# Row-prefix sums of eight batches: one static part for all batches, a ring of three instead of four, shorter programs

## The chip, the cores and the metric

One core of a Trainium2 chip runs the kernel. Its time is the device time of one execution, in microseconds (us). Five runs of the kernel before were timed; one further execution was taken by the hardware profiler, and all views below are of that one.

## The reference

```python
B, S, D = 8, 8192, 512                     # x: float32 [B, S, D], w: float32 [D, D]
mask = (pos < lengths[:, None, None])
cs = np.cumsum(x * mask, axis=1)
midpoints = (lengths // 2).clip(0)
mid_features = cs[b_idx, midpoints, :]      # one row per batch
return np.matmul(mid_features[:, None, :], w).squeeze(1)
```

Only one row of the running sum is used per batch, so what has to be computed is the sum of the rows 0 to min(length // 2, length - 1) of each batch, and then a product of eight rows with w. The lengths are data: the kernel learns at run time how many rows each batch needs. In the draw that is timed they are 1138, 5379, 511, 4113, 1809, 7542, 7716 and 1140, so that half of each is 569, 2689, 255, 2056, 904, 3771, 3858 and 570.

## The kernel before

The sum over rows is a matrix product. A chunk is a tile of 128 partitions, each with U = 8 consecutive rows of some batch (a unit, 16 KB). For each of the 8 rows (a slab, u) TensorE multiplies the tile's 128 x 512 values with a 128 x 8 table of ones and zeros, which says to which batch the partition's row belongs and whether it counts. The products of all chunks are added up in one PSUM bank, `s_ps`, in four groups of columns (32 j), one for every fourth slab. They are folded together at the end.

Rows come in three ways. The *front* (L519) is static: rows 0 to 255 of all batches, two parts of four batches with 2 MB each, issued by SP before anything is known of the lengths, into slots 0 and 1 of the ring `xt`. The *gathers* are dynamic: POOL's `fetch` (L244) loads by a table of unit numbers, `idx`, one chunk of 128 units (2 MB) at a time. A unit number that is out of range moves no bytes. The *back* (L281, `xb`) is static again: rows 256 to 511 of batches 0 and 1, loaded at the end. So batches 0 and 1 begin their gathered rows at 512 and the other six at 256; the rows `least`, `extra`, `jump` and `shift` carry this difference through the arithmetic on DVE (L317 to L329). The last gather goes in two halves to a buffer of its own, `xl`.

The order at the start, on DVE (`vector`, L297): constants, then from the lengths a row of unit counts (`row`), which PE spreads over the partitions by a product with ones (L441, `bc_ps`); from that the table of unit numbers (`ge`, `z`, `idx`) for all C = 31 possible chunks; then a second row (`row2`) and its spread (`b2_ps`), the weights of the front, and the weights `wc` of all chunks (`early`, `wc`). PE (`tensor`, L427) first writes zeros into its PSUM banks by products with a row of zeros (L437).

The steady state is a ring of R = 4 slots. SP relays (`relay`): once a slot's weights (`s_wr`) and its gather (`s_full`) are there it raises `s_rdy`, on which PE waits. After a chunk's eight products PE raises `s_done`. On that, POOL (`gather`, L266) copies the next column of `idx` into `now` and issues the next gather into the freed slot, and ACT (`weigh`) copies the next chunk's weights into `wr`. Behind each chunk PE runs two idle products (L449), whose result nobody reads. The front parts stand in slots 0 and 1, the first two gathers go to slots 2 and 3 without waiting for any chunk.

At the end POOL issues the two halves of the last chunk, `xb` and `w` in this order (L279 to L288), on one queue. PE (`pe_end`, L472) adds the last chunk, then `xb` into `c_ps` (two batches, quarter by quarter of the columns), folds `s_sb` into `mf_ps` (L495, four products), adds `c_sb` by a product with `pick` (L498), and multiplies by w (`o_ps`). DVE and ACT copy the result out; SP and ACT store it. PE's program has `pe_end` first in memory, then 56 waits that are met at once (`pe_pad`), then its start.

Every DVE operation is recorded at L301, all of PE's slab products at L429; the tile names tell them apart.

Of the kernel before, what the change touches and what calls it, by code (L numbers as in the profile page):

```python
# [8 lines left out]
I32 = mybir.dt.int32  # L9
# [6 lines left out]
def kernel(  # L16
# [13 lines left out]

    nc = tc.nc
# [5 lines left out]
    R = 4  # L37
    UB = S // U
    HEAD = 256
    FRONT = 2  # L40
    FB = B // FRONT
    BB = 2
    BU = 2
    BACK = slice(HEAD, HEAD + P * BU)
    HU, BKU = HEAD // U, (BACK.stop - HEAD) // U
# [3 lines left out]
    PAD = 56  # L49
    HALF = 2  # L50
    UH = U // HALF
    xu = x.rearrange("b (q u) d -> (b q) (u d)", u=U)
    xh = x.rearrange("b (q u) d -> (b q) (u d)", u=UH)
# [10 lines left out]
    def sem(name):  # L64
# [3 lines left out]
    xl = sb("xl", [P, HALF, UH * D])  # L68
    xb = sb("xb", [P, BB, BU * D])
    wt = sb("wt", [P, KC, D])  # L70
    lens = sb("lens", [1, 2 * B], I32)
    l16 = sb("l16", [1, B], I32)
    l2 = sb("l2", [1, B], I32)
    least = sb("least", [1, B])
    extra = sb("extra", [1, B])
    jump = sb("jump", [1, B - 1])
    shift = sb("shift", [1, B])
    last = sb("last", [1, B])
# [5 lines left out]
    chunks = sb("chunks", [1, 1], I32)  # L84
    ones = sb("ones", [1, P])
    zero = sb("zero", [1, D])
    p_i = sb("p_i", [P, 1], I32)
    p4 = sb("p4", [P, 1], I32)
    base = sb("base", [P, 1], I32)
    rank = sb("rank", [P, 1])  # L90
    rank8 = sb("rank8", [P, 1])
    q_i = sb("q_i", [P, C], I32)
    v_i = sb("v_i", [P, C * U], I32)
    u_i = sb("u_i", [P, U], I32)
    h_i = sb("h_i", [P, FB], I32)
    h_f = sb("h_f", [P, FB], I32)
    off_f = sb("off_f", [P, FB])
    at_f = sb("at_f", [P, FB])
    v_f = sb("v_f", [P, U, FB])
    v_b = sb("v_b", [P, BU], I32)  # L100
    v8 = sb("v8", [P, C * U])
# [3 lines left out]
    idx_h = sb("idx_h", [P, HALF], I32)  # L105
    now = sb("now", [P, R], I32)
    early = sb("early", [P, C, U, B])
    wc = sb("wc", [P, C, U * B])
    wr = sb("wr", [P, R * U * B])
    wl = sb("wl", [P, U * B])  # L110
    wb = sb("wb", [P, BB, BU, BB])
    fold_i = sb("fold_i", [P, B], I32)
    fold_m = sb("fold_m", [P, B], I32)
    fold = sb("fold", [P, B])
    pick_i = sb("pick_i", [P, KC, BB], I32)
    pick = sb("pick", [P, KC, B])
    s_sb = sb("s_sb", [P, D])
    c_sb = sb("c_sb", [P, P])
# [4 lines left out]
    c_ps = ps("c_ps", [P, D])  # L123
    mf_ps = ps("mf_ps", [P, KC * B])
    o_ps = ps("o_ps", [P, D])
# [5 lines left out]
    s_front = [sem(f"front{k}") for k in range(FRONT)]  # L131
    s_last = [sem(f"last{k}") for k in range(HALF)]
    s_back = [sem(f"back{k}") for k in range(BB)]
    s_w = [sem(f"w{k}") for k in range(4)]
    s_len, s_out, s_pool, s_dve, s_pe, s_done, s_wr, s_rdy, s_zero, s_act, s_wl, s_now = (
        sem(n) for n in ("len", "out", "pool", "dve", "pe", "done", "wr", "rdy", "zero", "act", "wl", "now"))
# [3 lines left out]
    QUARTERS = [slice(0, D // 2, 2), slice(1, D // 2, 2), slice(2 * P, 3 * P), slice(3 * P, D)]  # L140
    W_AT = (0, 2)

    def weights_of(s):
        return wr[:, s * U * B:(s + 1) * U * B]
# [12 lines left out]
    def sync(sp):  # L157
# [5 lines left out]
        sp.wait_ge(s_dve, marks["chunks"])  # L163
        sp.load(left, chunks[:])
        sp.wait_ge(s_dve, marks["front"])
        for f in range(FRONT):
            sp.wait_ge(s_front[f], 16)
            sp.sem_inc(s_rdy, 1)
        sp.br(f"sy_0_{FRONT}")

        def relay(s):
            sp.wait_ge(s_wr, have)
            sp.wait_ge(s_full[s], full)
            sp.sem_inc(s_rdy, 1)
            sp.reg_add(have, have, 1)
            if s == FRONT - 1:
                sp.reg_add(full, full, 16)

        ring(sp, "sy", left, relay)
        with nc.body("sy_end", valid_engines=[sp.engine]):  # L180
            sp.wait_ge(s_dve, marks["out0"])
            sp.wait_ge(s_act, 1)
            store(sp, 0)
            sp.br(END)


    def scalar(act):
        act.memzero(xl[:]).then_inc(s_zero, 1)  # L188
        left = act.alloc_register("left_act")
        free = act.alloc_register("free_act")  # L190
        act.wait_ge(s_dve, marks["w"])
        act.load(left, count[:])
        act.reg_sub(left, left, 1)
        last = act.snap(left)
        act.copy(out=wl[:], in_=wc[:, bass.ds(last, 1)].rearrange("p c e -> p (c e)"),
                 ).then_inc(s_wl, 1)
        act.reg_add(left, left, FRONT)
        for s in range(FRONT, R):
            act.copy(out=weights_of(s), in_=wc[:, s - FRONT]).then_inc(s_wr, 1)
        act.reg_sub(left, left, R)  # L200
        act.reg_mov(free, 1)
        act.br("ac_0_0")

        def weigh(s):
            act.wait_ge(s_done, free)
            col = act.snap(free)
            act.copy(out=weights_of(s),  # L207
                     in_=wc[:, bass.ds(col + (R - FRONT - 1), 1)].rearrange("p c e -> p (c e)"),
                     ).then_inc(s_wr, 1)
            act.reg_add(free, free, 1)  # L210

        ring(act, "ac", left, weigh)
        with nc.body("ac_end", valid_engines=[act.engine]):
            for g in range(2):
                act.wait_ge(s_pe, 6 + g)
                act.copy(out=o_sb[64 * g:64 * g + B, P:], in_=o_ps[64 * g + 32:64 * g + 32 + B, :P],  # L216
                         ).then_inc(s_act, 1)
            act.wait_ge(s_act, 2)
# [8 lines left out]
    def gpsimd(pool):  # L227
        pool.iota(p_i[:], pattern=[[0, 1]], base=0, channel_multiplier=1).then_inc(s_pool, 1)
        pool.wait_ge(s_pool, 1)
        for k in range(4):  # L230
            pool.iota(base[32 * k:32 * k + 32], pattern=[[0, 1]],
# [3 lines left out]
        pool.iota(q_i[:], pattern=[[P, C]], base=0, channel_multiplier=0).then_inc(s_pool, 1)  # L235
        pool.iota(h_i[:], pattern=[[-1, FB]], base=4 * FB, channel_multiplier=1)
        pool.iota(u_i[:], pattern=[[1, U]], base=0, channel_multiplier=0)
        pool.iota(v_i[:], pattern=[[P * U, C], [1, U]], base=HEAD, channel_multiplier=0)
        pool.iota(v_b[:], pattern=[[1, BU]], base=BACK.start, channel_multiplier=BU)
        pool.iota(fold_i[:], pattern=[[-1, B]], base=128, channel_multiplier=1)  # L240
        pool.iota(pick_i[:], pattern=[[-32, KC], [-1, BB]], base=0, channel_multiplier=1,
# [8 lines left out]
        n = pool.alloc_register("n_pool")  # L250
        free = pool.alloc_register("free_pool")
        pool.wait_ge(s_dve, marks["idx"])
        pool.load(n, count[:])
        pool.reg_sub(n, n, 1)
        pool.reg_mov(free, 1)
        pool.br("gp_a_0")
        for c in range(R - FRONT):
            with nc.body(f"gp_a_{c}", valid_engines=[pool.engine]):
                pool.br_cmp(n, c, f"gp_b_{c}", "gp_end", "IS_GT")
            with nc.body(f"gp_b_{c}", valid_engines=[pool.engine]):  # L260
                fetch(xt[:, c + FRONT], xu, idx[:, c:c + 1], B * UB, s_full[c + FRONT])
                if c + 1 == R - FRONT:
                    pool.reg_sub(n, n, R - FRONT)
                pool.br(f"gp_a_{c + 1}" if c + 1 < R - FRONT else "gp_0_0")

        def gather(s):  # L266
            pool.wait_ge(s_done, free)
            col = pool.snap(free)
            pool.tensor_copy(out=now[:, s:s + 1], in_=idx[:, bass.ds(col + (R - FRONT - 1), 1)],  # L269
                             ).then_inc(s_now, 1)  # L270
            pool.sem_inc(s_now, -1)._wait_ge(s_now, 1)  # L271
            fetch(xt[:, s], xu, now[:, s:s + 1], B * UB, s_full[s])
            pool.reg_add(free, free, 1)  # L273

        ring(pool, "gp", n, gather)
        with nc.body("gp_end", valid_engines=[pool.engine]):
            pool.wait_ge(s_zero, 1)
            pool.wait_ge(s_dve, marks["idx_h"])
            for h in range(HALF):  # L279
                fetch(xl[:, h], xh, idx_h[:, h:h + 1], B * S // UH, s_last[h])  # L280
            for b in range(BB):  # L281
                pool.dma_start(out=xb[:, b], in_=x[b, BACK].rearrange("(q u) d -> q (u d)", u=BU),  # L282
                               ).then_inc(s_back[b], 16)
# [13 lines left out]
    def vector(dve):  # L297
# [16 lines left out]
        fill(zero[:], 0)  # L314
        fill(ones[:], 1)
        mark("ones")
        fill(least[:, BB:], 0)  # L317
        fill(least[:, :BB], BKU)
        fill(extra[:, :1], 0)
        fill(extra[:, 1:BB], -BKU)  # L320
        fill(extra[:, BB:], 0)
        fill(jump[:, :BB - 1], UB + BKU)
        fill(jump[:, BB - 1:], UB)
        fill(shift[:, :1], 0)
        fill(shift[:, 1:BB], -BKU * U)
        fill(shift[:, BB:], 0)
        fill(row[:, :1], -BKU)
        fill(row[:, B + 1:B + 2], HU + BKU)
        fill(row[:, 2 * B + 1:], FAR)  # L329
        dve.wait_ge(s_pool, 1)  # L330
        step(ts, out=p4[:], in0=p_i[:], scalar1=2, scalar2=None, op0=ALU.logical_shift_right)
        dve.wait_ge(s_pool, 6)
        step(stt, out=rank[:], in0=p4[:], scalar=-63.0, in1=base[:], op0=ALU.mult, op1=ALU.add)
        step(ts, out=z[:, :, B + 1], in0=q_i[:], scalar1=rank[:], scalar2=None, op0=ALU.add)
# [3 lines left out]
        step(stt, out=mm_[:], in0=l16[:], scalar=float(1 - HU), in1=least[:], op0=ALU.add,  # L338
             op1=ALU.max)
        step(dve.tensor_tensor_scan, out=row[:, 1:B + 1], data0=extra[:], data1=mm_[:],  # L340
# [221 lines left out]
```

## Time and profile before

| what | value |
|---|---|
| five runs | 82.68 to 83.46 us, median 82.99 |
| the profiled execution | 82.86 us, of which 81.1 us span from first to last instruction |
| PE | busy 57.6 us (71%), weight loads 15.3 |
| DVE | busy 14.1 us (17%) |
| ACT | busy 8.1 us (10%) |
| POOL | busy 20.7 us (26%) |
| DMA | 31.25 MB, 385 GB/s over the span |
| front, issue to landing | 11.0 us median, two transfers of 2048 KB |
| ring gathers, issue to landing | 16.0 us median, nine of them |
| xb, issue to landing | 18.4 us median |
| instruction fetches by DMA in the span | one on queue 8, two on queue 14, 0.02 MB each queue |

The profile's page cuts the span in 40 slices of about 2.03 us. In the row of a unit a digit is its busy share in tenths, 9 being 90% or more. The chain of waits follows what ended last back to what released it. Matmul records of one 32-bit product come in pairs, so a chunk's eight products are 16 records. In the rows of groups, "x" counts instructions, and the time behind the bar is busy time and the mean of one.

### The profile page before, as it was taken

Reading aid. Unit: us, or ns where it says so; the run is one execution under the profiler, and the core shown is the slowest. Engines: PE = TensorE matmul, PEld = TensorE weight load, DVE = VectorE, ACT = ScalarE, POOL = GpSimd, SP = SyncE. Lnnn points to the kernel's source line nnn. Section 1 sums busy time; section 2 is a strip of 40 time slices with the busy share of each in tenths; the row PEclk is TensorE's granted clock in tenths of the full one; section 3 lists DMA queues with packets and bytes.
Section 4 is the critical chain, followed back from the end, with each engine's and each line's share of the span. In section 5 each row is a group of like instructions: output and inputs, shape, how many; then the busy total and the mean of one; then the engine's idle time right before and its main releaser. Section 6 shows DMA issues by size and latency. Waiting matters only on the chain. (4 is left out here: it accounts for less than half of the span.)

```text
span 81.1 us, 1123 instructions
## 1 busy us (share of the span) xinstructions
PE 57.6 (71%) x358; PEld 15.3 (19%) x358; DVE 14.1 (17%) x58; ACT 8.1 (10%) x16; POOL 20.7 (26%) x44
## 2 busy tenths in 40 slices
PE   1962399999939669395894939759395793848840
PEld 1462121121102021120211202011020211104620
DVE  4738899610000000000000000000000000004220
ACT  2991000310100101000010100100000000000020
POOL 4400642515050410505023050369900000000000
PEclk9999999999999999999999999999999999999995
DMA  0899998999999999999999999999999999999600
GB/s 0 315 453 388 453 445 372 412 436 416 412 469 412 412 469 408 412 469 412 412 461 428 396 445 436 412 436 445 412 420 453 420 388 428 404 410 408 224 2 6
DMA packets 2805, 31.25 MB, mean 385 GB/s; under 512 B 386, under 2 KB 402, under 8 KB 914
## 3 DMA queue, kind: packets, MB, share of 16 engines
q0 software_dynamic: 2480, 27.00, 79.0%
q1 hardware_dynamic: 304, 4.20, 12.5%
q8 instruction: 1, 0.02, 0.1%
q14 instruction: 2, 0.02, 0.0%
q10 hardware_dynamic: 18, 0.01, 0.0%
HBM read 31.46 MB, written 0.02 MB: 388 GB/s over the span
## 5 line engine op out<-in xcount | busy, mean ns | idle before, releaser
L429 PE MATMUL s_ps<-xt,wr 128*8 128x512 f32 x208 | 26.4, 628 | 14.4 <-PEq L458 14.2
L449 PE MATMUL idle_ps<-rank,v_f 128*4 128x512 f32 x48 | 23.3, 608 | 0.0
L429 PEld LDWEIGHTS s_ps<-xt,wr 128*8 128x8 f32 x208 | 5.0, 90 | 34.2 <-issue 34.2
L245 POOL DMA_INDIRECT xt<-in_x_dram,now x9 | 9.2, 1021 | 8.0 <-POOLq L271 8.0
L301 DVE COPY s_sb<-s_ps 128x256 f32<-128x256 f32 x2 | 0.8, 424 | 57.2 <-PE s_ps L429 57.1
L269 POOL COPY now<-idx 128x1 int32 x9 | 2.2, 241 | 22.7 <-PE s_ps L429 22.7
L449 PEld LDWEIGHTS idle_ps<-rank,v_f 128*4 128x4 f32 x48 | 4.3, 89 | 17.5 <-issue 17.5
L207 ACT COPY wr<-wc 128x64 f32 x9 | 2.2, 244 | 33.2 <-PE s_ps L429 33.0
L245 POOL DMA_INDIRECT xt<-in_x_dram,idx x2 | 2.2, 1120 | 5.8 <-DVE at_f L301 5.5
L188 ACT ACTIVATE xl<-xl 128x4096 uint32<-128x4096 uint32 x1 | 3.6, 3617 | 0.0
L437 PE MATMUL s_ps<-zero 1*128 1x512 f32 x2 | 2.1, 1137 | 1.8 <-DVE jump L301 1.8
L216 ACT COPY o_sb<-o_ps 8x128 f32<-8x128 f32 x2 | 0.5, 257 | 26.7 <-PE o_ps L429 26.7
L429 PE MATMUL s_ps<-xl,wl 128*8 128x512 f32 x16 | 2.1, 594 | 1.3 <-DMA xl<-in_x_dram,idx_h 1.3
L441 PE MATMUL b_ps<-row,ones 1*128 1x16 f32 x2 | 0.6, 381 | 2.3 <-DVE row L301 2.3
L301 DVE TENSOR_TENSOR wc<-early,ge 128x1984 f32<-128x1984 f32 x1 | 2.2, 2224 | 0.0
L301 DVE TENSOR_TENSOR early<-v,b_ps 128x1984 f32<-128x1984 f32 x1 | 2.2, 2221 | 0.0
L245 POOL DMA_INDIRECT xl<-in_x_dram,idx_h x2 | 2.0, 992 | 0.6 <-issue 0.6
L429 PE MATMUL c_ps<-xb,wb 128*2 128x128 f32 x32 | 1.3, 276 | 0.3 <-DMA xb<-in_x_dram 0.2
L429 PE MATMUL o_ps<-wt,mf_sb 128*8 128x128 f32 x32 | 1.2, 273 | 0.3 <-DVE mf_sb L301 0.3
L188 ACT ACT_TABLE_LOAD x1 | 1.3, 1283 | 1.5 <-SPq L56 1.5
L495 PE MATMUL mf_ps<-fold,s_sb 128*128 128x8 f32 x8 | 1.3, 265 | 0.0
L495 PEld LDWEIGHTS mf_ps<-fold,s_sb 128*128 128x128 f32 x8 | 1.1, 193 | 0.5 <-issue 0.2
(75 smaller groups left out, 23.7 us busy)
## 6 DMA issues: line engine op xcount, KB each, us to landing
xt<-in_x_dram SPq DMA_DIRECT2D x2, 2048.0 KB, 11.0
xb<-in_x_dram POOLq DMA_DIRECT2D x2, 512.0 KB, 18.4
wt<-in_w_dram POOLq DMA_DIRECT2D x1, 512.0 KB, 19.5
wt<-in_w_dram POOLq DMA_DIRECT2D x1, 256.0 KB, 19.6
wt<-in_w_dram POOLq DMA_DIRECT2D x2, 128.0 KB, 19.3
xt<-in_x_dram,now POOLq DMA_INDIRECT x9, 16.0
xt<-in_x_dram,idx POOLq DMA_INDIRECT x2, 12.3
xl<-in_x_dram,idx_h POOLq DMA_INDIRECT x2, 17.3
```

What stands on the lines that cost most here:

```text
L188: act.memzero(xl[:]).then_inc(s_zero, 1)
L207: act.copy(out=weights_of(s), in_=wc[:, bass.ds(col + (R - FRONT - 1), 1)].rearrange("p c e -> p (c e)"),).then_inc(s_wr, 1)
L216: act.copy(out=o_sb[64 * g:64 * g + B, P:], in_=o_ps[64 * g + 32:64 * g + 32 + B, :P],).then_inc(s_act, 1)
L245: pool.indirect_dma_start(out=to, out_offset=None, in_=units, in_offset=bass.IndirectOffsetOnAxis(ap=at, axis=0), bounds_check=n - 1, oob_ ...
L269: pool.tensor_copy(out=now[:, s:s + 1], in_=idx[:, bass.ds(col + (R - FRONT - 1), 1)],).then_inc(s_now, 1)
L301: do(*args, **kw).then_inc(s_dve, 1)
L429: return pe.matmul(to[32 * j:32 * j + weights.shape[1], :rows.shape[1]], lhsT=weights, rhs=rows, start=False, stop=False, skip_group_check ...
L437: pe.matmul(to[:, :width], lhsT=zero[:, :P], rhs=zero[:, :width], start=True, stop=False, skip_group_check=True)
L441: pe.matmul(to[:, :of.shape[1]], lhsT=ones[:], rhs=of[:], start=True, stop=True,).then_inc(s_pe, 1)
L449: pe.matmul(idle_ps[:FB], lhsT=v_f[:, 0], rhs=rank[:].to_broadcast((P, D)), start=True, stop=True, skip_group_check=True)
L495: pe.matmul(mf_ps[:, B * k:B * (k + 1)], lhsT=s_sb[:, at], rhs=fold[:], start=False, stop=False, skip_group_check=True)
```

## The change

All batches are treated alike: the front is rows 64 to 255 of all batches (two parts, four batches each, 6 rows per partition, 1.5 MB), rows 0 to 63 of all batches are loaded last, just ahead of w, and gathered rows begin at 256 everywhere. The four correction rows on DVE go. The ring has three slots; the front parts stand in slots 1 and 2, gather 0 goes to slot 0 at once, gathers 1 and 2 wait for the front part that holds their slot. The last gather is an ordinary chunk.

The table of unit numbers and the weights are made for the first three chunks first and for the rest later. The column of unit numbers of a chunk (`now`) is copied by ACT instead of POOL, and POOL no longer loads the count ahead of its first gather. ACT writes the zeros: the part of the ring's slots 1 and 2 that the front leaves out, and the five PSUM banks. PE's zero products go. Behind each of the two row broadcasts PE now runs one idle product, behind each chunk two, but none behind the last two. PE's loop ends are shared (`pe_next`, `pe_more`, `pe_to`), the closing part stands last in memory, and the padding is gone. The rows at the end go to `d_ps` in two column halves; ACT copies them; `mf_ps` is two banks, each closed by its own product.

```diff
-    R = 4
+    R = 3
-    HEAD = 256
-    FRONT = 2
+    TOP, HEAD = 64, 256
+    PARTS = 2
...
+    FU, BU = FB * (HEAD - TOP) // P, FB * TOP // P
...
     def scalar(act):
-        act.memzero(xl[:]).then_inc(s_zero, 1)
+        act.memzero(xt[:, 1:, FU * D:]).then_inc(s_zero, 1)
+        for bank in (s_ps, d_ps, *mf_ps, o_ps):
+            act.memzero(bank[:]).then_inc(s_zero, 1)
...
         def weigh(s):
-            act.wait_ge(s_done, free)
-            col = act.snap(free)
+            act.wait_ge(s_done, turn)
+            c = act.snap(turn)
+            act.copy(out=now[:, s:s + 1], in_=idx[:, bass.ds(c, 1)]).then_inc(s_now, 1)
+            act.wait_ge(s_dve, marks["w"])
...
+            act.wait_ge(s_pe, 3)
+            for at in (slice(0, P), slice(P, 2 * P)):
+                act.copy(out=d_sb[:, at], in_=d_ps[:, at]).then_inc(s_act, 1)
...
         pool.wait_ge(s_dve, marks["idx"])
-        pool.load(n, count[:])
...
+                if c > 0:
+                    pool.wait_ge(s_done, c)
+                fetch(xt[:, c], xu, now[:, c:c + 1], B * UB, s_full[c])
+                if c == 0:
+                    pool.load(left, count[:])
...
         def gather(s):
-            pool.wait_ge(s_done, free)
-            col = pool.snap(free)
-            pool.tensor_copy(out=now[:, s:s + 1], in_=idx[:, bass.ds(col + (R - FRONT - 1), 1)],
-                             ).then_inc(s_now, 1)
             pool.sem_inc(s_now, -1)._wait_ge(s_now, 1)
             fetch(xt[:, s], xu, now[:, s:s + 1], B * UB, s_full[s])
...
+            for f in range(PARTS):
+                pool.dma_start(out=xb[:, f], in_=x[FB * f:FB * (f + 1), :TOP].rearrange(
+                    "b (q u) d -> q b (u d)", u=BU)).then_inc(s_back[f], 16)
...
+        table(now[:], 0, R, B + 1)
         mark("idx")
...
+        weights(0, R)
+        mark("w0")
+        table(idx[:, R:], R, C, B + 2)
+        mark("table")
...
+        dve.wait_ge(s_done, PARTS)
+        weights(R, C)
         mark("w")
...
             for name, to, of in (("row", bc_ps, row), ("row2", b2_ps, row2)):
-                pe.wait_ge(s_dve, marks[name])
-                pe.matmul(to[:, :of.shape[1]], lhsT=ones[:], rhs=of[:], start=True, stop=True,
-                          ).then_inc(s_pe, 1)
+                pe.matmul(to[:, :of.shape[1]], lhsT=ones[:1], rhs=of[:], start=True, stop=True,
+                          )._wait_ge(s_dve, marks[name]).then_inc(s_pe, 1)
+                idle(1)
...
+        with nc.body("pe_next", valid_engines=[pe.engine]):
+            pe.reg_sub(left, left, 1)
+            pe.br_cmp(left, -PARTS, "pe_more", "pe_end", "IS_GT")
+        with nc.body("pe_more", valid_engines=[pe.engine]):
+            pe.br_cmp(left, 1 - PARTS, "pe_idle", "pe_to", "IS_GT")
+        with nc.body("pe_idle", valid_engines=[pe.engine]):
+            idle(IDLE)
+            pe.br("pe_to")
...
+            for f in range(PARTS):
+                pe.wait_ge(s_back[f], 16)
+                for u in range(BU):
+                    at = (R * U + f * BU + u) * B
+                    for h in range(2):
+                        mm = add(d_ps, 2 * u + h, ww[:, at:at + B],
+                                 xb[:, f, u * D + h:(u + 1) * D:2])
             mm.then_inc(s_pe, 1)
+            for i in range(2):
+                pe.wait_ge(s_dve, marks[f"s{i}"])
+                for k in (2 * i, 2 * i + 1):
+                    pe.matmul(mf_ps[i][:, B * (k % 2):B * (k % 2 + 1)], lhsT=s_sb[:, QUARTERS[k]], rhs=fold[:],
+                              start=False, stop=False, skip_group_check=True)
+                pe.wait_ge(s_act, i + 1)
+                pe.matmul(mf_ps[i][:], lhsT=d_sb[:, i * P:(i + 1) * P],
+                          rhs=fold2[:].rearrange("p h b -> p (h b)"), start=False, stop=True,
+                          skip_group_check=True).then_inc(s_pe, 1)
...
-        with nc.body("pe_pad", valid_engines=[pe.engine]):
-            for _ in range(PAD):
-                pe.wait_ge(s_dve, 1)
-            pe.br("pe_0")
...
+    for f in range(PARTS):
+        nc.sync.dma_start(out=xt[:, f + 1, :FU * D], in_=x[FB * f:FB * (f + 1), TOP:HEAD].rearrange(
+            "b (q u) d -> q b (u d)", u=FU)).then_inc(s_front[f], 16)
```

## The prediction

> **What bounds the kernel now.** I read the page's slices first, then the queues, the chain of waits, and the timeline of the two ends. One unit counts below: a share of the 16 DMA engines.
>
> ```profile
> DMA  0899998999999999999999999999999999999600
> GB/s 0 315 453 388 453 445 372 412 436 416 412 469 412 412 469 408 412 469 412 412 461 428 396 445 436 412 436 445 412 420 453 420 388 428 404 410 408 224 2 6
> ...
> q0 software_dynamic: 2480, 27.00, 79.0%
> q1 hardware_dynamic: 304, 4.20, 12.5%
> q8 instruction: 1, 0.02, 0.1%
> ...
> DMA xb<-in_x_dram 23%; POOL xl L245 2%; PE o_ps L429 1%; PE c_ps L429 1%; DVE o_sb L301 1%; POOL xb L282 1%; PE mf_ps L495 1%; PE mf_ps L498 0%; DVE mf_sb L301 0%; POOL xt L245 0%; POOLq L245 0%; POOLq L149 0%; POOLq L273 0%
> ```
>
> From the second slice to the last but three (2.2 to 76.5 us) the DMA engines are never idle. 31.2 MB in those 74 us is 421 GB/s; the stretch 20 to 30 us alone shows 433. So the kernel is a stream, with 2.2 us ahead of it and a tail of compute behind. The chain ends in the landing of xb (issued at 56.27, landed 18.71 us later, at 74.98). What the change is worth is read at four places only: the bytes, the stream's start, gaps in it, and the tail.
>
> **Bytes.** The draw's lengths need, beyond the static rows, 1520 units of 8 rows (16 KB) before, 1584 after. Before: 4.19 MB front + 1.05 MB xb + 24.90 MB. After: 3.15 + 1.05 + 25.95. Both are 30.15 MB, and w is 1.05 in each: nothing is gained or lost. The last gather shrinks from 112 units in two halves to 48 units in one.
>
> **The stream's start.** SP issues the front at 0.97 in both programs, nothing stands before it: 0. The front is now 3.15 MB and is followed by chunk 0 (2.10 MB), so at 420 GB/s the engines run dry 5.24 / 0.42 = 12.5 us after 2.3, at 14.8, unless chunk 1 is queued. Chunk 1 shares its slot with the first front part and waits for PE (s_done 1). Before, 8.3 MB could be queued without any wait. The new wait, step by step:
>
> - lengths: DVE takes them at 3.00, straight behind other work, so they had landed by then; four small operations of 0.19 (3.00 to 3.73) give row at 3.7. The PE zero products (1.81 to 5.0) no longer stand before the row broadcast; ACT writes the zeros instead (before: 4096 columns in 3.62 us; now 2048, 1.8, and five banks, some 0.3 each: done by 6.5).
> - row broadcast 3.8 + 0.6 = 4.4, beside p4, z, up_i, count on DVE. The table for three columns: three operations of about 0.25 instead of 0.45 to 0.48, so "idx" at 5.4 (before: 6.88). POOL's first gather no longer waits for the register load that lay between 6.88 and 8.55: about 5.8. Earlier by 2.7, worth nothing, as the front feeds the engines until 9.8.
> - row2 is ready at 6.0; the new idle product (two cold records of 0.86) ends at 6.1 to 6.2; row2's broadcast to 6.8; the four static weights to 7.6. The front's first part (half of 3.15 MB, at 2.3 + 3.7 + landing) is there by about 6.7. PE then runs the second idle product to 8.5 and the first part.
>
> ```profile
> 8.55 1.21 POOL L245 DMA_INDIRECT xt<-in_x_dram,idx  x1 [5.52 <-DVE at_f L301]
> ...
> 9.55 3.60 PE L429 MATMUL s_ps<-xt,wr 128*8 128x512 f32 x16 [1.25 <-PEq L458]
> ...
> 15.60 1.90 PE L429 MATMUL s_ps<-xt,wr 128*8 128x512 f32 x16
> ```
>
> The same 16 records take 3.60 us cold and 1.90 warm. In this trace the slow records last from 9.55 to about 14.3, 4.7 us of unbroken work. The Trainium skill ("TensorE: Matmul & The Clock Gate", Part 1: The HAM clock gate) states a warm-up of about 3.4 us of busy time. After the change PE is busy from 3.8 on. By the rule it is warm at 7.2, and the part takes 8.5 to 10.4; by the row it is warm at 8.5 to 9, the same within 0.3; if it stays cold, 12.0. I take the row: s_done 1 at 10.6. POOL's gather (1.02) is out at 11.8. What then passes until bytes move the trace shows only under a busy stream; between 0 and the 2.7 us from the end of the first gather's issue (9.76) to the end of the front. So data of chunk 1 from 11.8 to 14.5: no gap. All cold: 13.2 to 15.9, a gap up to 1.1.
>
> **Gaps in the ring of three.** In the trace a chunk of 2.10 MB takes 4.88 us. From its last byte to PE 0.6, PE 1.9. Before, POOL copied the index column itself, 0.18 with 0.88 of semaphore wait (starts 17.98 and 19.04), then gathered 1.02. Now ACT copies (its old copy began 0.4 after PE's end, 0.24) and POOL only gathers: 0.6 + 1.9 + 0.4 + 0.3 + 1.0 = 4.2 after landing, plus 0 to 2.7: at most 6.9. Two further chunks lie queued, 9.8 us. The engines do not end a chunk together (about 1.4 us between first and last in the trace's packets), so 8.4 count. Slack at least 1.5: no gap. The deeper ring was not used for its depth: "xt<-in_x_dram,now", issue to landing 16.0 us, becomes about 11. Idle products behind each chunk stay at two (1.7 us warm), so PE needs 3.6 of 4.88. Chunk weights: the three first at 8.9, the rest (two operations of 2.0, behind s_done 2) by about 18; chunk 3, their first user, lands near 25. All hidden.
>
> **The stream's own length.** The 8 KB halves of xl cost 0.313 us each against 0.611 for 16 KB: 14 of them per engine against 7, 0.1 us. Page q8 shows one 16 KB instruction fetch, 0.1% of 16 x 81.1 = 1.3 us, on one engine at 2.2 us; one packet of that size is 0.6 us of it that data could have used. PE's program shrinks from 91 products to 60 (four instructions each: 364 to 240), POOL's loop bodies by half. If fetches vanish, the engine that ends last ends earlier, but the next lags by 0.1 and the third by 0.5 us: gain 0 to 0.5, I take 0.3. Together -0.4.
>
> **The tail.**
>
> ```profile
> 75.03 0.64 PE c_ps L429 x12
> 75.67 0.54 PE mf_ps L495 x4
> 76.21 0.30 PE mf_ps L498 x2
> 76.51 0.02 issue
> 76.53 0.20 DVE mf_sb L301
> 76.74 0.04 issue
> 76.78 1.07 PE o_ps L429 x28
> 77.85 0.02 issue
> 77.88 0.28 DVE o_sb L301
> ```
>
> Now, from xb's landing to the first o_sb copy, 2.90 us: 0.05 + 0.64, half of s_sb's products, pick, copy, o_ps. After: the last four d_ps products (half as many, twice as wide) 0.60; ACT copies d_sb 0.26 (from its o_sb row, 257 ns) + 0.05; the d product of half 0 0.30; the two s products of half 1 0.54, in order behind it; d product of half 1 0.30; o_ps 1.07, whose first half hides half 1's DVE copy. With starts 3.15: +0.25 (0, if the s products slip under the ACT copies, to +0.45, if the second ACT copy is late). PE reaches d_ps in time: chunk 12 (48 units, 1.8 us of stream, full 1.9 of PE) ends about 0.6 before xb's landing, and no idle products stand behind chunks 11 and 12. The DVE copies of s_sb fit there. w, last as before, lands after xb by the same bytes; o_ps's fourth row of w is needed 0.3 later than now.
>
> **Sum against the profiled run** (82.86, span 81.1): 0 + 0 - 0.4 + 0.25 = -0.15, or 82.7. The median of the five runs is 0.13 above the profiled one: **82.8**. About 0.5% (0.41 us) is what a measurement of this kernel tells from no change.
>
> **Rivals.**
>
> - Faster, 82.3 (0.26): all fetches vanish (-0.6 with the halves) and the tail's order costs nothing or gains 0.1. For: the page has three instruction fetches. Against: four products in a row depend on ACT's copies.
> - Slower by a dry stream, 84.0 (0.16): the refills come too late. At the start, a cold PE and the full 2.7 us of gather latency leave 1.1 us; it decides when s_done 1 comes later than 11.1 (14.8 - 1.02 - 2.7). In the ring it decides when landing-to-refill exceeds 8.4 us; each of ten refills would then pay its excess. For: the queue loses a third of its depth. Against: the sums above.
> - Slower by a code fetch in the tail, 84.1 (0.08): a rule against the change, "Runtime: NRT & Kernel Launch", Instruction fetch mechanics: a taken branch to a page outside the current two stalls for its fetch; pages are 16 KB, 256 instructions. The change adds branches behind every chunk and puts the closing products last, where PE's 240 product instructions and its control pass the first page. The nearest row is q8's 1.3 us. By the row the sum is 84.1 if it happens beside o_ps; by the rule the second page is inside the window and costs 0. I take 0: loops stay in one page.
> - Slower by the tail alone, over 83.4 (0.06): +0.45 there and no fetch gained.
>
> The rest (0.44) is the forecast within 0.5%; its own range is 82.4 to 83.4. Slower in all 0.30, faster 0.26. Range for 8 in 10: 82.2 to 84.0.
>
> **What would show it.** Right: DMA slices full from the second to the last but three; first gather near 5.8; the first front part at 1.9 to 2.6 us of PE; gathers landing 10 to 12 us after issue; no q8 row; o_sb copies 3.0 to 3.3 us after xb lands. Wrong: a slice below 9 near 15 us (dry start), several along the run (ring), or a hole in PE inside o_ps (fetch).

## The result, and the profile after

The changed kernel takes 83.46 us (median of 42 runs) against 83.04 (79 runs of the kernel before): ratio 1.0052, 95% interval 1.0036 to 1.0068. It is slower by about 0.5%, where 82.8 and "no change" had been forecast.

The profiled execution of the changed kernel took 83.32 us, its span is 80.6. Before, these were 82.86 and 81.1. So **the kernel proper became shorter by 0.5 us, and what lies around it longer by 0.94**: time minus span was 1.77 and is 2.71. Over all compared runs the medians are 81.3 and 1.80 before (in the 55 runs beside the first four experiments), 80.6 and 2.83 after.

In the tables below, "rest" is time minus span. Numbers of an experiment are medians of its fast runs; of a_pad4 and a_pad5 more than half of the runs lie some 2 us higher and are left out, so of these two only the rest is used below, which is 1.73 to 2.00 in all of their runs.

The page of the changed kernel, slices and queues (a digit is a slice's DMA share in tenths; the queue rows give packets, MB, share of 16 engines):

```profile
DMA  0899999999999999999999999999999999999700
...
q0 software_dynamic: 2480, 28.05, 82.3%
q1 hardware_dynamic: 304, 3.15, 9.6%
q8 instruction: 1, 0.02, 0.1%
q10 hardware_dynamic: 18, 0.01, 0.0%
q14 instruction: 1, 0.00, 0.0%
```

The stream has no gap: the slices are full from the third to the last but three, and the bytes have only moved between the queues. Queue 14, which the experiments below show to fetch code for the engines other than PE, had two packets in the kernel before:

```profile
q14 instruction: 2, 0.02, 0.0%
```

It now has none of that size within the span. That looks like a gain on the profile's page. It is where the loss is: the fetches did not vanish, they moved behind the end of the span, where the profile's page does not count them.

The start, from the timeline:

```profile
2.13 0.16 DVE L275 TENSOR_SCALAR l<-lens 1x8 int32<-1x8 int32 x1 [0.85 <-DMA lens<-in_lengths_dram]
...
5.61 1.19 POOL L227 DMA_INDIRECT xt<-in_x_dram,now  x1 [2.80 <-DVE ww L275]
...
7.37 3.15 PE L399 MATMUL s_ps<-xt,ww 128*8 128x512 f32 x16
...
11.39 1.02 POOL L227 DMA_INDIRECT xt<-in_x_dram,now  x1 [4.60 <-PE s_ps L399]
```

The lengths are there at 2.13, POOL gathers at 5.61 instead of 8.55, PE takes the first front part from 7.37 and is still slow, and the second gather is out at 12.41, ahead of 14.8, when the front and the first gather run out.

The tail, from the chain of waits:

```profile
65.06 9.16 DMA xb<-in_x_dram
74.23 0.04 issue
74.27 0.64 PE d_ps L399 x8
74.91 0.57 PE mf_ps L450 x4
75.48 0.23 PE mf_ps L453 x2
75.71 0.46 PE mf_ps L450 x4
76.17 0.23 PE mf_ps L453 x2
76.40 1.00 PE o_ps L399 x32
77.40 0.02 issue
77.42 0.28 DVE o_sb L275
```

xb lands at 74.23, 0.75 earlier than before; from there to the first o_sb copy it takes 3.19 us instead of 2.90.

### The profile page after: what moved, and what is told of

The parts are those of the page before. It is cut to its first block, busy times and chain, and to the rows that moved or that the text cites. A ratio compares the mean times of both kernels' runs of the same rounds, so it can differ in the third digit from the quotient of the medians.

```text
span 80.6 us, 1184 instructions
## 1 busy us (share of the span) xinstructions
PE 59.7 (74%) x360; PEld 14.5 (18%) x360; DVE 12.4 (15%) x44; ACT 10.1 (13%) x34; POOL 18.0 (22%) x31
## 3 DMA queue, kind: packets, MB, share of 16 engines
q1 hardware_dynamic: 304, 3.15, 9.6%
## 5 line engine op out<-in xcount | busy, mean ns | idle before, releaser
L399 PE MATMUL s_ps<-xt,ww 128*8 128x512 f32 x240 | 30.3, 614 | 14.7 <-PEq L419 14.7
L405 PE MATMUL idle_ps<-ones 128*4 128x512 f32 x56 | 28.2, 624 | 0.0
L227 POOL DMA_INDIRECT xt<-in_x_dram,now x13 | 13.1, 1006 | 48.6 <-POOLq L250 38.8
L399 PEld LDWEIGHTS s_ps<-xt,ww 128*8 128x8 f32 x240 | 6.3, 90 | 38.3 <-issue 38.3
L405 PEld LDWEIGHTS idle_ps<-ones 128*4 128x4 f32 x56 | 4.7, 87 | 17.9 <-issue 17.8
L187 ACT COPY now<-idx 128x1 int32 x10 | 1.9, 191 | 44.5 <-PE s_ps L399 40.5
L275 DVE TENSOR_TENSOR early<-v_f,b_ps 128x192 f32<-128x192 f32 (+1 forms) x2 | 2.4, 1188 | 4.3 <-PE s_ps L399 4.2
L189 ACT COPY ww<-wc 128x64 f32 x10 | 2.4, 244 | 0.0
L275 DVE TENSOR_TENSOR wc<-early,ge 128x192 f32<-128x192 f32 (+1 forms) x2 | 2.4, 1193 | 0.1
L168 ACT ACTIVATE xt<-xt 128x2048 uint32<-128x2048 uint32 x1 | 1.9, 1909 | 0.0
## 6 DMA issues: line engine op xcount, KB each, us to landing
xt<-in_x_dram,now POOLq DMA_INDIRECT x13, 11.1
```

What stands on the lines that cost most here:

```text
L168: act.memzero(xt[:, 1:, FU * D:]).then_inc(s_zero, 1)
L187: act.copy(out=now[:, s:s + 1], in_=idx[:, bass.ds(c, 1)]).then_inc(s_now, 1)
L189: act.copy(out=weights_of(s), in_=wc[:, bass.ds(c, 1)].rearrange("p c e -> p (c e)"),).then_inc(s_wr, 1)
L227: pool.indirect_dma_start(out=to, out_offset=None, in_=units, in_offset=bass.IndirectOffsetOnAxis(ap=at, axis=0), bounds_check=n - 1, oob_ ...
L275: do(*args, **kw).then_inc(s_dve, 1)
L399: return pe.matmul(to[32 * j:32 * j + weights.shape[1], :rows.shape[1]], lhsT=weights, rhs=rows, start=False, stop=False, skip_group_check ...
```

## The experiments

The trace keeps more than the page counts: the DMA packets and the semaphore events behind the last counted instruction. Zero is the span's start here; the expectations below count packet times from 0.25 us earlier, so "76.8" there is 76.5 here, and so on. What they show, in us:

| | before | changed |
|---|---|---|
| code fetches (KB) after the start | 2.23 (16), 18.88 (8), 30.96 (8) | 76.53 (16), 82.30 (8), 83.18 (8) |
| span's end | 81.09 | 80.61 |
| closing exchange between the engines, first to second event | 0.10 | 0.50 |
| the same, fourth-last to third-last event | 0.04 | 0.32 |
| last event to the end of the time, counted from the span's start | -0.13 | 0.12 |

The closing exchange is the run of semaphore events with which the five engines end the program, 14 of them; the first comes 0.54 us after the span in both kernels. Three of its steps are longer: 0.40 + 0.28 + 0.25 = 0.93 us, which is the whole loss around the span. The 16 KB packet runs on queue 8, PE's; the 8 KB ones on queue 14. A code page here is the piece of program that one such packet brings. **Theory B: programs that have become shorter reach the end of their code page behind the kernel instead of inside it, and the exchange waits for the next page.** The rivals: PE's page does it (A); or the rest has nothing to do with code (C).

### Whose page

With never executed instructions ahead of it, a program reaches the end of its code page sooner. The register is always 0:

```diff
-        eng.br(f"{name}_0")
+        eng.br(f"{name}_e")
...
+            with nc.body(f"{name}_e", valid_engines=[eng.engine]):
+                never = eng.alloc_register(f"never_{name}")
+                eng.reg_mov(never, 0)
+                eng.br_cmp(never, 0, f"{name}_skip", f"{name}_0", "IS_GT")
+            with nc.body(f"{name}_skip", valid_engines=[eng.engine]):
+                for _ in range(80):
+                    eng.wait_ge(s_dve, 1)
+                eng.br(f"{name}_0")
```

The expectations count two such waits as one instruction. For PE there are 448 waits, with the comparison in place of its first branch.

> The changed kernel, with 224 instructions that are never executed placed ahead of PE's program, so that PE enters its second code page at its start, as in the kernel before. The changed kernel's span is 0.5 us shorter than before, but its time lies 2.8 us over its span instead of 1.8. Theory A (PE's code page, fetched at 76.8 us on queue 8, delays the end of the program behind the span): time minus span falls from 2.8 to 1.8, time 82.4; the 16 KB fetch moves to the first 4 us. Theory B (the pages of the other engines): 2.8 stays, 83.4. Rival C (the time behind the span has nothing to do with code pages): 2.8 stays here and in the two following runs.

> The changed kernel, with 40 never executed instructions (and a branch around them) ahead of the programs of DVE, SP, ACT and POOL, PE as it is. Theory B (the two 8 KB code fetches behind the span, at 82.6 and 83.4 us, are what the end waits for): the fetches move into the stream, time minus span 1.8, time 82.4 to 82.6. Theory A: 2.8 and 83.4. Rival C: 2.8.

> Both paddings. A or B alone: as the better of the two, 82.4 to 82.6. If each costs a part: time minus span falls here further than in either. Rival C: 2.8, 83.4.

And in the kernel before, the padding taken out. It stands behind a branch that is never taken, so its waits are not met at once but jumped over:

```diff
-            for _ in range(PAD):
-                pe.wait_ge(s_dve, 1)
```

> The kernel before without its 28 never executed padding instructions in PE's program; nothing else changes. Theory A, if the padding is what holds PE's page boundary at the start: time minus span grows from 1.8 towards 2.8, time 83.4 to 84. Theory B: time minus span stays at 1.8, 83.0. Rival C: 1.8, 83.0.

Then one engine at a time, as in a_pad4, to tell one late page as the whole cause (B1) from several that each cost a part (B2):

> The changed kernel with the 40 never executed instructions on DVE alone. Theory B1 (one engine's late 8 KB code page is the whole of the 1.0 us behind the span): in exactly one of the four single paddings time minus span falls from 2.8 to 1.8, in the three others it stays at 2.8. Theory B2 (each late page costs a part): it falls by a part in two or more of them. For DVE: 1.8 if it is the engine whose page arrives last, 83.4 us and 2.8 if not. DVE's page would come while DVE has slack, so the span should stay near 80.6 and the time near 82.5 in the good case.

> The same on POOL alone. B1: 1.8 or 2.8, not between. With all four paddings a code page fetched in the stream put the second gather off from 11.4 to 12.7 us and the DMA rate fell to 303 to 393 GB/s from 14 to 22 us: if it is POOL's page, the span grows here to 82 to 83.5 in part of the runs, and in none of the other three.

> The same on ACT alone. B1: time minus span 1.8 or 2.8. ACT hands the column of unit numbers to POOL from chunk 3 on, so a page that comes late in the stream could put off one gather by some 0.5 us, which the queue covers: span 80.6 to 81.0.

> The same on SP alone. B1: time minus span 1.8 or 2.8. SP relays every chunk to PE; a page fetched in the stream would put off one relay, span 80.6 to 81.5.

| run | time | span | rest | ratio to before, interval |
|---|---|---|---|---|
| kernel before, beside the first four (beside the last four the same to 0.01) | 83.09 | 81.3 | 1.80 | |
| a_padpe | 84.53 | 81.8 | 2.67 | 1.018 (1.011 to 1.025) |
| a_pad4 | 83.00 | 81.1 | 1.82 | 0.9995 (0.996 to 1.003) |
| a_pad5 | 83.64 | 81.8 | 1.90 | 1.006 (1.002 to 1.011) |
| b_nopad | 83.22 | 81.4 | 1.80 | 1.002 (0.9995 to 1.004) |
| a_pad_dv | 83.63 | 81.3 | 2.37 | 1.007 (1.005 to 1.009) |
| a_pad_gp | 83.06 | 80.9 | 2.20 | 1.002 (0.9995 to 1.005) |
| a_pad_ac | 83.40 | 80.9 | 2.49 | 1.003 (1.000 to 1.005) |
| a_pad_sy | 83.41 | 80.6 | 2.80 | 1.004 (1.001 to 1.006) |

PE's page leaves the rest at 2.67, the others' bring it to 1.82: theory A and rival C fall. b_nopad agrees: PE's packet comes later (4.58 instead of 2.23), the rest stays. It is not one engine (B1) but several that each cost a part (B2), and the events tell which part is whose. In a_pad_dv the 0.50 between the first two events is 0.10 again, and the last step is 0.10 longer. In a_pad_gp the 0.32 becomes 0.04, and the last step is -0.13 as before, although ACT's program is as it was. In a_pad_ac the last step alone goes, to -0.10. So two parts add up, DVE's and POOL's, and ACT's page costs something only while POOL's is late. To move DVE's and POOL's alone was not tried. SP's page costs nothing: its stretch puts a third 8 KB packet behind the span (82.23 and 82.33, where the changed kernel has one at 82.30), and the rest stays. The expectation that POOL's page would lengthen the span to 82 to 83.5 was wrong.

How the exchange loses the time stays open. The packets at 82.30 and 83.18 begin only after the two longer steps have ended, at 81.66 and 83.12, so it is not these packets that the steps wait for; and there are two packets where three engines are concerned. What the runs show is that each step goes when the end of that engine's code page is moved.

The padded kernels don't win, since their spans grow; 82.4 to 82.6 had been expected. a_padpe, where all theories had missed the longer span, shows why most plainly. PE's 16 KB packet, at 76.53 in the changed kernel, comes at 2.26, as in the kernel before (2.23). The queue row and the chain of a_padpe's profile:

```profile
q8 instruction: 2, 0.03, 0.2%
...
65.88 9.15 DMA xb<-in_x_dram
75.04 0.04 issue
```

xb lands at 75.03, 0.8 later than in the changed kernel, with the same data plan; by the medians its span is 1.2 longer. A landing waits for the last of 16 DMA engines. The 16 signals with which the second half of xb lands come between 73.71 and 74.98 in the kernel before, between 73.73 and 74.23 in the changed one, and between 73.69 and 75.04 in a_padpe: the first is the same, the last is not. In a_pad_dv, with one 8 KB packet in the stream, 15 signals come by 74.27 and one at 75.16. So code in the stream makes one engine late, and taking it out is most of what shortened the span. It is not all that spreads the signals: in a_best_s below, the profiled execution (82.83, its median is 82.28) has its last one at 74.67 without code in the stream, so the medians of the spans count for more than one trace.

### Where a page does not hurt

First ahead of the stream: larger stretches (156, 144 and 128 waits on DVE, ACT and POOL), so that the page is entered at the program's start.

> The changed kernel with larger never executed stretches ahead of the programs of DVE (78 instructions), ACT (72) and POOL (64), so that each enters its new code page at its start, about 1 us, ahead of the row stream (first bytes near 2.3 us). SP is left as it is, since its padding changed nothing. Theory B2 (late pages of DVE, ACT and POOL behind the span, each a part of 1.0 us) with the cost of a page fetched inside the stream as the reason why the single paddings lengthened the span by 0.3 to 0.7: span 80.6, time minus span 1.8, time 82.4 to 82.5, faster than before by 0.6. Rival (the padding itself, a branch and a longer way to the first instruction, lengthens the span, wherever the page comes): span 81.0 to 81.3, time 82.9 to 83.1. Second rival: pages[...] end again behind the kernel, so that the next late page takes the place of the old one: time minus span 2.2 to 2.8.

> The same on ACT and POOL only. B2: DVE's part stays, time minus span between 1.8 and 2.4, span 80.6. If the end waits for the last of the three only, DVE's late page holds it at 2.4 or above.

a_early3: 82.79, span 81.0, rest 1.77, ratio 0.998 (0.994 to 1.003). a_early2: 83.45, span 81.3, rest 2.16. The rest is as expected, the span is not: the packets came at 2.08 to 4.13, in the stream's first two microseconds and not ahead of it. The rival, that the padding itself lengthens the span, had forecast these spans too; a_pad_sy speaks against it, where the padding puts no packet in the stream and the span is 80.6.

Then behind the stream. The stretch stands at the end of the program, here ACT's; POOL has it behind a new wait, ahead of its wait for the stores:

```diff
             store(act, 1)
-            act.br(END)
+            never = act.alloc_register("never_ac")
+            act.reg_mov(never, 0)
+            act.br_cmp(never, 0, "ac_skip", END, "IS_GT")
+        with nc.body("ac_skip", valid_engines=[act.engine]):
+            for _ in range(80):
+                act.wait_ge(s_dve, 1)
+            act.br(END)
...
+            pool.wait_ge(s_pe, 6)
```

> The changed kernel with a never executed stretch of 40 instructions at the end of the programs of DVE, ACT and POOL instead of at their start (POOL's behind a wait for o_ps, ahead of its wait for the stores), so that each enters its new code page in the 3 us between o_ps and the landing of the stores, when no rows move any more. Theory (late pages behind the span cost 1.0 us, and a page fetched inside the row stream lengthens the span by 0.3 to 0.7): span 80.6 as in the changed kernel, time minus span 1.8 as before, time 82.4; the 8 KB fetches of queue 14 between 78.5 and 80.5 us. Rival (any stretch of skipped code costs what it saves): span 81.0 to 81.3. Second rival (3 us are too short, the pages come as late as now): time minus span above 2.2, 83.0 or more.

> The changed kernel as it is, on the same chip as the run before it: span 80.6, time minus span 2.8, time 83.4 to 83.5.

a_tail: 83.21, span 81.4, rest 1.78, ratio 1.003 (1.001 to 1.005). after_again: 83.20, span 80.45, rest 2.72, ratio 1.001 (0.9985 to 1.004), beside a kernel before of 82.96, 81.1 and 1.80, so on this chip the changed kernel is as fast as the one before, with the same shift from span to rest. In a_tail the loss has moved into the span. Its packets came at 78.53 to 79.72, and the 1 KB packets of the stores run from 78.48. So the three were tried singly, to tell whether the fetches meet the stores (D) or POOL stands still for its own page (E), and POOL's also with `pool.wait_ge(s_pe, 3)`, ahead of the stores:

> The changed kernel with the stretch at the end of POOL's program alone, behind a wait for o_ps. Theory D (a page fetched at 78.8 to 80.0 us lies on the same DMA engines as the 1 KB store packets, and puts the stores' landing off): time minus span falls by POOL's part, 0.6, to 2.2; the span grows by up to 1.0 only if this fetch meets the stores. Rival E (POOL itself, which waits for the stores, stands still for its own page): the span grows by 1.0 here and not in the two others.

> The same at the end of DVE's program alone, behind its last copy (78.0 us). D: time minus span 2.4, span longer by 0 to 1.0 as the fetch meets the stores or not. E: span 80.5, time minus span 2.4, time 82.9.

> The same at the end of ACT's program alone, behind its store's issue. D: time minus span 2.5, span longer by 0 to 1.0. E: span 80.5, time 83.0.

> As the first, but POOL enters the new page behind a wait for d_ps (74.9 us) instead of o_ps, so that its fetch comes near 76 us, when the last of w lands and the stores are 2 us away. D: span 80.5 to 80.8, time minus span 2.2, time 82.8, faster than the first. E: the same, since POOL has its page long before the stores land.

| run | code packet | time | span | rest | ratio, interval |
|---|---|---|---|---|---|
| kernel before, beside these | | 82.84 | 81.05 | 1.80 | |
| a_tail_gp | 78.96 | 83.23 | 81.0 | 2.22 | 1.005 (1.002 to 1.007) |
| a_tail_dv (four runs) | 78.59 | 83.78 | 81.4 | 2.35 | 1.012 (1.008 to 1.016) |
| a_tail_ac | 79.72 | 83.02 | 80.5 | 2.51 | 1.002 (1.0005 to 1.004) |
| a_tail_gp3 | 76.64 | 82.68 | 80.5 | 2.19 | 0.999 (0.997 to 1.001) |

Two of these side by side. The page's first line and the issue of the stores from the timeline, first a_tail_dv:

```profile
span 81.3 us, 1186 instructions
...
77.65 0.37 SPq L208 DMA_DIRECT2D out_dram<-o_sb  x1
77.99 0.55 ACTq L208 DMA_DIRECT2D out_dram<-o_sb  x1
```

and a_tail_ac:

```profile
span 80.5 us, 1186 instructions
...
77.67 0.37 SPq L214 DMA_DIRECT2D out_dram<-o_sb  x1
78.00 0.55 ACTq L214 DMA_DIRECT2D out_dram<-o_sb  x1
```

The stores are issued at the same moment, and one span is 0.8 longer. DVE has nothing to do with the stores by then; its packet lies at 78.59, among those of the stores, and ACT's at 79.72, behind them. The last signal of the stores' landing comes at 80.11 in a_tail_dv and at 79.34 in a_tail_ac. So it is the meeting on the DMA engines (D), not POOL standing still (E): POOL's page costs 0.5 of span behind o_ps and nothing behind d_ps.

The last two put all three pages between: POOL behind d_ps, ACT at its end, and DVE between its copies of mf_sb and o_sb, or behind those of s_sb.

```diff
             mark(f"mf{i}")
-        for g in range(2):
+        never = dve.alloc_register("never_dv")
+        dve.reg_mov(never, 0)
+        dve.br_cmp(never, 0, "dv_skip", "dv_fin", "IS_GT")
+        with nc.body("dv_skip", valid_engines=[dve.engine]):
+            for _ in range(96):
+                dve.wait_ge(s_dve, 1)
+            dve.br("dv_fin")
+        with nc.body("dv_fin", valid_engines=[dve.engine]):
+            for g in range(2):
```

> The changed kernel with all three pages entered between the stream and the stores: POOL behind d_ps (its fetch came at 76.9 us and cost no span), ACT at its end (79.97 us, no span), DVE between its copies of mf_sb and o_sb (entered at 76.6 us, so that the fetch comes near 77.5, ahead of the store packets at 78.7). D: span 80.5, time minus span 1.8, time 82.3 to 82.4, faster than the kernel before by 0.6 and than the changed one by 1.0. Rival (DVE stands still for its page at 76.6): o_sb copies and span later by up to 0.5, time 82.8.

> The same, but DVE enters its page behind the copies of s_sb (74.6 us), with the fetch near 75.5, inside the transfer of w, which has 0.5 us of slack. D: span 80.5 to 80.8, time 82.3 to 82.6. Rival (standing still): mf_sb copies later, as above.

a_best_mf: **82.31, span 80.5, rest 1.77, ratio 0.990 (0.985 to 0.995)**. a_best_s: 82.28, span 80.5, rest 1.74, ratio 0.991 (0.988 to 0.994). The kernel before beside them: 83.06, 81.25, 1.80. Both beat it, by 0.9 to 1.0%, and lie below both measurements of the changed kernel (83.46 and 83.20). Page and chain of a_best_mf:

```profile
span 80.5 us, 1190 instructions
...
q14 instruction: 3, 0.02, 0.1%
q8 instruction: 1, 0.02, 0.1%
...
76.32 1.00 PE o_ps L422 x32
77.32 0.02 issue
77.34 0.28 DVE o_sb L290
```

Queue 14 has its packets within the span again, at 76.08, 77.60 and 79.74. Between o_ps and the o_sb copy stands the same 0.02 of issue as in the changed kernel, so DVE did not stand still for its page inside the kernel. In the closing exchange the two steps are 0.10 and 0.04, and the last event lies 0.13 behind the time's end, as before.

## Why the prediction was wrong

**The bytes: right.** 31.2 MB before and after.

**The start: right in its outcome.** 0 was forecast, and no slice is short. On the way the lengths came 0.9 earlier than taken, and PE began the first part at 7.37 and not at 8.5, but it took 3.15 us and not 1.9 to 2.6. That s_done 1 came about 10.5 (10.6 forecast) is two misses that cancelled. The clock was granted in full from 9.8 on (records of 1.06 us before, of 0.59 after), 6.9 us after PE's unbroken work began at 2.93, not after the 4.7 of the row taken, nor the 3.4 of the rule; in a_early3, where PE's work begins alike, it came at 7.8. So this time differs from one execution to the next. The second gather was out at 12.41 (11.8 forecast), and the dry stream didn't come.

**The ring: right.** Gathers land 11.1 us after issue (forecast: about 11), and no refill was late.

**The tail: right in size, by some luck.** +0.29, forecast +0.25. Four products of s_sb (0.57) stood in the chain where a copy by ACT (0.31) had been put, and the other products took 0.25 less than forecast.

**The stream's own length: right in kind, too small.** -0.4 was forecast, 0.1 of it for the halves of xl; measured is -0.75 at the landing of xb. The term for a code fetch inside the stream, "0 to 0.5, I take 0.3", is worth about 0.65 here, by difference; a_padpe, which puts PE's page back, gives 0.8 by its trace and 1.2 by its median span. With the measured size the kernel proper would have come out at 81.1 - 0.75 + 0.29 = 80.6, which is the span measured.

**The step that failed is the sum's frame.** "Sum against the profiled run (82.86, span 81.1): 0 + 0 - 0.4 + 0.25" took the 1.77 us around the span as fixed, and the gain in "If fetches vanish" was booked without asking where they go. They went behind the span: 0.93 us, by DVE's and POOL's pages, ACT's having a share only beside POOL's. None of the rivals had this cost either. The forecast had the clue, since it counted PE's instructions and POOL's loop bodies, and it looked for a late page in PE and inside o_ps. PE's page did move to the tail (76.53) and cost nothing there (3.19 us from xb's landing to the first o_sb copy, and 3.20 in a_padpe, where no page of PE comes between); "no q8 row" was wrong. The rule cited from the Trainium skill ("Runtime: NRT & Kernel Launch", Instruction fetch mechanics) was applied to the kernel's branches alone; it also says that crossing a page boundary is mostly hidden. Measured, that holds inside the kernel where the packet meets nothing (a_best_mf), and not in the closing exchange (0.40, 0.28, 0.25) nor among rows (0.3 to 1.2 of span) or stores (0.5 to 0.9). Its 16 KB for a page is what queue 8 shows; the packets of queue 14 have 8 KB.

With these pages out of the way the same change gains 0.9 to 1.0% (a_best_mf, a_best_s). It isn't shown how an engine loses the time in the exchange, only that each longer step goes when that engine's page comes sooner. Nor is it shown why the spans of a_pad_gp and a_pad_ac grew by 0.3 and that of a_pad_dv by 0.7: one 8 KB packet in the stream (13.93, 21.72, 7.40) goes with each, but which engine carried it was not followed.

## What to carry to other kernels

Compare time minus span before explaining a change by the span: a shorter kernel can end in a longer close, and the profile's page shows nothing of it. Shorter programs move their page boundaries. In these runs a code fetch was free only where no row, no store and no closing exchange was near, and 40 to 48 never executed instructions were enough to put it there. In a stream that fills the DMA engines, the last engine sets the landing: here 16 KB of code on one of them, a packet of 1.1 us, cost 0.8 to 1.2 us of span, about as much as if all of them had waited for it.

## What was not expected of the hardware

- The exchange behind the kernel lasts 1.37 us from its first to its last event when all pages are there, and 2.05 in the changed kernel.
- An 8 KB code packet beside two stores of 8 KB put the end of the span off by 0.5 (POOL) and 0.9 us (DVE).
- Engines that jump over 64 to 78 instructions at their start, near 1 us, have their code packets at 2.1 to 4.1 us, so that in these runs the fetch did not come ahead of a stream that starts at 2.2.
